# State-space steps of a hybrid decoder layer on one Trainium2 core: two groups' steps taken as one

## The chip, the cores and the metric

The kernel runs on one core of a Trainium2 chip. The metric is the device time of one execution in microseconds (us). Times are medians of several executions; the profile is that of one execution, taken by the hardware profiler. The engines are called PE (matrix products), DVE (vector), ACT (activations), POOL (GpSimd) and SP (which issues most loads). Each takes its instructions in the order in which the program lists them; the weight loads of PE are shown apart, as PEld.

## What is computed

One layer of two parallel branches over a sequence of 1024 positions, width 1024, all in float32. The branch that matters here is a state-space mixer (Mamba-2's dual form) with 8 groups of 4 heads of 64 channels, 128 states and chunks of 128 positions:

```python
def ssd_scan(x, dt, a, bmat, cmat):
    ...
    cb = jnp.einsum('bclgn,bcsgn->bcgls', cc, bc)
    y_diag = jnp.einsum('bcgls,bcgrls,bcsgrp->bclgrp', cb, decay, xd)
    decay_to_end = jnp.exp(a_cs[..., -1:] - a_cs)
    chunk_states = jnp.einsum('bcsgn,bcgrs,bcsgrp->bcgrpn', bc, decay_to_end, xd).astype(jnp.float32)
    ...
    def step(state, inp):
        cs, cd = inp
        return state * cd[..., None, None] + cs, state
    ...
    y_off = jnp.einsum('bclgn,bcgrpn,bcgrl->bclgrp', cc, prev_states, jnp.exp(a_cs))
    return (y_diag + y_off).reshape(b, s, h, p).astype(x.dtype)
```

Afterwards `y_b + xh * d_skip` is multiplied by `silu(ssm_z)` and normed over each group's 256 channels. Both branches are projected, gated, summed, projected again, added to the input and normed.

## The kernel before

The program has one long run of large projections, then the state-space steps, then the projection of the state-space output and the last projection. Large products are done with operands split in a high and a low part (128x512 products of a special 32-bit float type), and with a scheme that needs seven block products for eight.

The change lies in the state-space steps. The work is cut in 32 **steps**: `order` lists them as (group g, piece s), groups in rounds of two, so that steps alternate between the two groups of a round: (0,0) (1,0) (0,1) (1,1) ... (1,3) (2,0) .... A step handles 256 positions, two chunks of 128. Its parts, and the names of tiles by which the profile's rows show them:

- `fetch`: two loads on SP's queue, `dcy` (cumulated decay exponents) and `sl` (the six strips of inputs).
- `mask`, then `decay`: ACT makes `ea` (two instructions), POOL masks `dcy` (an affine select over 128x1024), ACT takes eight exponentials of `dcy`.
- `prep`: PE makes `pc` (products C times B, and B transposed) and `px` (x transposed), eight instructions of 128x128. DVE multiplies `dcy` by `pc` and makes `xd` and `xe` from `px`; ACT copies `bn` out of `pc`.
- `front`: PE does the eight products inside the chunk, `yi`, from `dcy` and `xd` (64-column tiles), and the increments of the state, `sp`, from `xe` and `bn` (one product a chunk). DVE adds the first increment to the state (`add_state`), makes `y` out of `yi` and the skip term (two instructions), and adds the second increment. POOL scales the state before each addition (`mul_state`).
- `back`: PE does the products with states, `yn`. DVE multiplies them by `ea` into `ym`, POOL adds `ym` to `y` and multiplies by the gate strip into `yz`.
- Every second piece of a group, `post` stores `yz`, ACT squares it (`squares`), POOL adds the two strips (`sum`), PE adds over channels with four products of 32-column tiles, `pq` (`post2`), and POOL later takes the root of a small tile `ssq` (`root`).

The last piece of a group (s=3) makes one increment instead of two, and the first (s=0) has no state to scale for its first chunk, so its `ym` and first POOL addition cover half as much.

The other branch's projection, 192 pairs of 128x512 products into `pma`, is the **filler**: `draw(n)` puts n pairs at a place in PE's order. Its evacuations (`tha`) and the low parts of its weights (`wal`) are DVE work that the scheduler places itself.

PE's products keep the order in which the code is written. On DVE, ACT and POOL the helper `link` ties each instruction of a step to the one before it on that engine, so the code's order is the engine's order there too; the other work falls between. All products land in eight PSUM banks of 128x512; the helper `bank` hands out two of them from one ring and six from another, of which the filler's pair holds two for as long as one output block lasts. A bank is written again when the last reader of its former tile is done.

Each step n of the loop before is: `front(n)`; a call that has ACT take the decays of step n+2, POOL scale the state of step n+1 and mask step n+3, and at most one task "beside" (`sum` or `root`); four or five pairs of filler; `back(n)`; `prep(n+2)`; `fetch`.

Of the kernel before, what the change touches and what calls it, by code (L numbers as in the profile page):

```python
# [35 lines left out]
def hybrid_kernel(  # L36
# [1036 lines left out]
    work, last = [], {}  # L1073
# [19 lines left out]
    class Group:  # L1093
# [40 lines left out]
        def prep(self, s):  # L1134
# [10 lines left out]
            xs = []  # L1145
            d3 = dcy.rearrange("p h i l -> p h (i l)")
            link("V", lambda: V.tensor_tensor(d3, d3, pc[:, 0:256].unsqueeze(1).to_broadcast([P, HPG, 256]), op=ALU.mult))  # L1147
            for v, f in (("xd", dthq), ("xe", dde)):
                t = p2x.tile([P, 512], F32, name=f"{v}{nm}", tag=v, bufs=3)
                link("V", lambda: V.tensor_tensor(t.rearrange("p (i h w) -> p i h w", i=2, h=HPG), x4,  # L1150
                                    fac(f, g, s).unsqueeze(3).to_broadcast([P, 2, HPG, HD]), op=ALU.mult))
                xs.append(t)
            bn = p2x.tile([P, 256], F32, name=f"bn{nm}", tag="bn", bufs=3)
            link("A", lambda: A.copy(bn, pc[:, 256:512]))  # L1154
            self.pre[s] = (sl, dcy, bn, xs[0], xs[1], ea)

        def front(self, s):

            g, nm = self.g, f"{self.g}_{s}"
            sl, dcy, bn, xd, xe, ea = self.pre[s]  # L1160
            yi = bank(f"yi{nm}")
# [5 lines left out]
            sp = bank(f"sp{nm}")  # L1167
            two = s < NCH // 2 - 1
            self.sts = [self.st]
            for i in range(2 if two else 1):  # L1170
                mm(sp[:, i * 256 : (i + 1) * 256], bn[:, i * P : (i + 1) * P], xe[:, i * 256 : (i + 1) * 256])
            self.add_state(s, 0, sp)
            if two:
                self.mul_state(s, 1)
            y1 = turn(y1_r, f"y1{nm}", F32).rearrange("p (j t) -> p j t", j=2)
            for j in range(2):
                link("V", lambda: V.scalar_tensor_tensor(y1[:, j], sl[:, 2 + j], dskt[:, 2 * g + j : 2 * g + j + 1],
                                           yi[:, j * 256 : (j + 1) * 256], op0=ALU.mult, op1=ALU.add))
            self.y[s] = y1
            if two:  # L1180
                self.add_state(s, 1, sp)
# [10 lines left out]
        def add_state(self, s, i, sp):  # L1192
# [35 lines left out]
        def post(self, q):  # L1228
# [5 lines left out]
            if g < NG - 2 or q == 0:  # L1234
                later(8, self.squares, q, [yz[:, j] for j in range(2)])
            else:
                self.late = [yz[:, j] for j in range(2)]
                later(5, self.late_squares)
# [12 lines left out]
        def sum(self, q, sq):  # L1251
            link("G", lambda: G.tensor_add(sq[0], sq[0], sq[1]))
            later(3, self.post2, q, sq[:1])
# [58 lines left out]

    def start_ssd():
        fetch(2)
        for n in range(2):
            later(3 + 5 * n, masks, n + 1)
            later(4 + 5 * n, decays, n + 1)
            g, s = order[n]
            later(13 + n, groups[g].prep, s)
# [202 lines left out]
    def ahead_of(n):  # L1522

        with tc.high_priority():
            decays(n + 3)
            if n + 1 < len(order) and order[n + 1][1]:
                groups[order[n + 1][0]].mul_state(order[n + 1][1], 0)
            for _ in range(1 if n < 29 else 2):
                beside_step()
            masks(n + 4)  # L1530

    def step(n, *fs):
        for f in fs:
            item(getattr(groups[order[n][0]], f), order[n][1])

    draw(6)
    for n in range(2):
        step(n, "front")
        ahead_of(n)
        draw(10)  # L1540
    for n in range(len(order)):
        if n > 1:
            step(n, "front")
            ahead_of(n)
            draw(6 if n == 2 else 4 + n % 2)
        step(n, "back")
        if n == 1:
            draw(4)
        if n + 2 < len(order):
            step(n + 2, "prep")  # L1550
        fetch(n + 6)
    while tasks or work:
        draw(2)
        run_tasks()
        beside_step()

# [232 lines left out]
    for u, (nm, k) in enumerate(units):  # L1789
        if k == 0:  # L1790
            if nm == "p1":
                first = {t: psb.tile([P, 512], F32, name=f"{t}p", tag=f"b{t}") for t in ('y1', 'x0', 'x1', 'y3', 'y0', 'x2', 'x3', 'y2')}
# [224 lines left out]
```

## Time and profile before

| What | Value |
| --- | --- |
| Median of 3 executions | 1373.79 us (1373.0 to 1373.83) |
| The profiled execution's own time | 1372.68 us |
| Its span, first to last instruction | 1370.7 us |
| Granted clock of PE | 0.999 |
| PE busy | 1356.4 us |
| Where the 32 steps lie | about 907 to 1118 us |

The profile's page gives the busy time of each engine; "idle before" in a row is how long the engine stood still before the instruction, and the arrow names what ended the wait. In a timeline, rows give start and duration; consecutive instructions of PE, DVE and POOL overlap a little at their ends (the next one starts before the last one's shown end), so what an instruction costs its engine is read from one start to the next.

### The profile page before, as it was taken

Reading aid. Unit: us, or ns where it says so; the run is one execution under the profiler, and the core shown is the slowest. Engines: PE = TensorE matmul, PEld = TensorE weight load, DVE = VectorE, ACT = ScalarE, POOL = GpSimd, SP = SyncE. Lnnn points to the kernel's source line nnn. Section 1 sums busy time; section 2 is a strip of 40 time slices with the busy share of each in tenths; the row PEclk is TensorE's granted clock in tenths of the full one; section 3 lists DMA queues with packets and bytes.
Section 4 is the critical chain, followed back from the end, with each engine's and each line's share of the span. In section 5 each row is a group of like instructions: output and inputs, shape, how many; then the busy total and the mean of one; then the engine's idle time right before and its main releaser. Section 6 shows DMA issues by size and latency. Waiting matters only on the chain.

```text
span 1370.7 us, 20173 instructions
## 1 busy us (share of the span) xinstructions
PE 1356.4 (99%) x6943; PEld 1114.6 (81%) x6943; DVE 1045.6 (76%) x1716; ACT 799.7 (58%) x1447; POOL 192.0 (14%) x191
## 2 busy tenths in 40 slices
PE   8999999999999999999999999999999999999997
PEld 7688888888888888888888888888888878788886
DVE  4786876777778889688897787468878856959976
ACT  5764656666657666466576665486867733333443
POOL 1000000000000000000000000016888871000002
PEclk9999999999999999999999999999999999999999
DMA  9675444333344657777666775489889858978913
GB/s 287 179 234 150 136 123 124 100 122 117 115 132 138 206 172 233 252 239 230 194 198 186 231 239 168 154 314 300 300 284 314 290 203 295 334 267 321 382 38 123
DMA packets 249530, 288.65 MB, mean 211 GB/s; under 512 B 16812, under 2 KB 196436, under 8 KB 249428
## 3 DMA queue, kind: packets, MB, share of 16 engines
q1 hardware_dynamic: 174868, 203.80, 46.3%
q10 hardware_dynamic: 74560, 83.57, 17.9%
q8 instruction: 55, 0.90, 0.3%
q14 instruction: 47, 0.39, 0.1%
HBM read 199.82 MB, written 87.49 MB: 210 GB/s over the span
## 4 chain that ended last, share of the span: by engine, by line
PE 87%; DVE 4%; DMA 3%; POOL 3%; ACT 1%; issue 1%; SPq 1%; POOLq 0%; ACTq 0%; DVEq 0%
PE xcb L565 6%; PE xz L565 6%; PE xx L565 6%; PE xuz L565 6%; PE xg L565 6%; PE pma L82 4%; PE ox L1861 3%; PE yuz L565 3%; PE ycb L565 3%; PE yp L1670 3%; PE yz L565 3%; PE vx L954 3%; PE yx L565 3%; PE yg L565 3%; PE yi L82 2%; PE sp L82 2%
## 5 line engine op out<-in xcount | busy, mean ns | idle before, releaser
L1123 POOL TENSOR_SCALAR_AFFINE_SELECT dcy<-dcy 128x1024 f32<-128x1024 f32 x32 | 35.4, 1106 | 791.5 <-DMA yl<-ya_d 747.2
L1131 ACT ACTIVATE dcy<-dcy,nacs 128x128 f32<-128x128 f32 x256 | 78.3, 389 | 3.6 <-POOL dcy L1123 3.2
L1147 DVE TENSOR_TENSOR dcy<-dcy,pc 128x1024 f32<-128x1024 f32 x32 | 39.0, 1219 | 9.2 <-PE pc L85 5.2
L1226 POOL TENSOR_TENSOR yz<-y,sl 128x512 f32<-128x512 f32 x32 | 43.8, 1369 | 2.5
L82 PE MATMUL pma<-yh,wah 128*128 128x512 f32 x128 | 42.7, 415 | 0.0
L82 PE MATMUL pma<-yh,wal 128*128 128x512 f32 x128 | 42.3, 412 | 0.0
L1154 ACT COPY bn<-pc 128x256 f32<-128x256 f32 x32 | 11.9, 371 | 50.7 <-DVE dcy L1147 48.3
L82 PE MATMUL pma<-yl,wah 128*128 128x512 f32 x128 | 40.1, 394 | 0.0
L1608 DVE SCALAR_TENSOR_TENSOR yn<-yn,par,rb 128x512 f32<-128x512 f32 x32 | 24.3, 760 | 20.6 <-DMA yn<-yb_d 18.8
L1119 ACT ACTIVATE ea<-dcy 64x512 f32<-64x512 f32 x64 | 39.8, 622 | 0.4
L1024 ACT ACTIVATE ac<-ac 128x1024 f32<-128x1024 f32 x32 | 33.9, 1060 | 9.4 <-DVE ac L1022 9.2
L1225 POOL TENSOR_TENSOR y<-y,ym 128x512 f32<-128x512 f32 (+1 forms) x32 | 37.4, 1169 | 2.1 <-DVE ym L1223 2.1
L1223 DVE TENSOR_TENSOR ym<-yn,ea 128x512 f32<-128x512 f32 (+1 forms) x32 | 19.9, 621 | 21.7 <-PE yn L82 21.7
L1022 DVE SCALAR_TENSOR_TENSOR ac<-c2x,cwt,ac 128x1023 f32<-128x1023 f32 (+2 forms) x24 | 30.7, 1279 | 6.3 <-ACT ac L1020 6.2
L82 PE MATMUL yi<-dcy,xd 128*64 128x128 f32 x512 | 35.0, 279 | 0.0
L1022 DVE SCALAR_TENSOR_TENSOR ac<-c2cb,cwt,ac 128x1023 f32<-128x1023 f32 (+2 forms) x24 | 30.6, 1275 | 5.6 <-ACT ac L1020 5.5
L1876 POOL TENSOR_TENSOR r<-r,fnw 128x512 f32<-128x512 f32 x4 | 5.3, 1345 | 206.3 <-ACT junk L1874 206.3
L986 ACT ACTIVATE vm<-vm,vr 128x128 f32<-128x128 f32 x64 | 25.8, 483 | 13.6 <-DMA vm<-v_d 13.1
L824 ACT CAST wbb<-wbr 128x512 fp32r<-128x512 f32 x32 | 19.8, 619 | 22.2 <-DMA wb_d<-wbb 16.2
L82 PE MATMUL sp<-xe,bn 128*128 128x256 f32 x112 | 32.7, 409 | 0.0
L82 PEld LDWEIGHTS yn<-sl,st 128*128 128x128 f32 x224 | 29.8, 191 | 2.8 <-POOL st L1189 0.4
L82 PEld LDWEIGHTS yi<-dcy,xd 128*64 128x64 f32 x512 | 27.3, 136 | 5.7 <-issue 2.9
(2963 smaller groups left out, 4372.6 us busy)
## 6 DMA issues: line engine op xcount, KB each, us to landing
sl<-s_d SPq DMA_DIRECT2D x32, 768.0 KB
s_d<-ac ACTq DMA_DIRECT2D x32, 512.0 KB
wb_d<-wbb ACTq DMA_DIRECT2D x32, 512.0 KB
dcy<-acs_d SPq DMA_DIRECT2D x32, 512.0 KB
av<-in_w_in_dram SPq DMA_DIRECT2D x36, 256.0 KB
aw<-in_ada_w_dram SPq DMA_DIRECT2D x16, 512.0 KB
wbr<-in_w_proj_b_dram SPq DMA_DIRECT2D x32, 256.0 KB
yb_d<-yz ACTq DMA_DIRECT2D x32, 256.0 KB
```

Of the source, the lines that this page charges most:

```text
L82: pin(PE.matmul(acc, l, r, start=first, stop=last))
L565: pin(PE.matmul(ps, lw[:, k * P : (k + 1) * P], r[k], start=first and n + k == 0, stop=n == 2 and k == 3, skip_group_check=not first))
L954: pin(PE.matmul(ps[pn][j], l[:, j * P : (j + 1) * P], r, start=nm in ("p1", "p5", "p2") and n + units[i][1] == 0, stop=n == 2 and k == 3, ...
L1022: V.scalar_tensor_tensor(ac[:, s:], cc[:, : S - s], conv_wt[:, 3 - s, i : i + 1], ac[:, s:], op0=ALU.mult, op1=ALU.add)
L1119: link("A", lambda: A.activation(ea[hh * HD : (hh + 1) * HD], dcy.rearrange("p (j e) i l -> p e j (i l)", e=2)[hh * HD : (hh + 1) * HD, hh ...
L1123: link("G", lambda: G.affine_select(out=d8, in_=d8, compare_op=ALU.is_ge, fill=-1e30, base=0, pattern=[[0, 2 * HPG], [1, P]], channel_mult ...
L1131: link("A", lambda: A.activation(dcy[:, h, i, :], dcy[:, h, i, :], AF.Exp, bias=sub[:, i, h : h + 1]))
L1147: link("V", lambda: V.tensor_tensor(d3, d3, pc[:, 0:256].unsqueeze(1).to_broadcast([P, HPG, 256]), op=ALU.mult))
L1225: link("G", lambda: G.tensor_add(y1[:, :, t0:], y1[:, :, t0:], m[:, :, t0:]))
L1226: link("G", lambda: G.tensor_mul(yz, y1, sl[:, 4:6]))
L1670: pin(PE.matmul(ps[j], a[:, v, js], r, start=first and n + k == 0, stop=n == 2 and k == KT - 1, skip_group_check=not first))
L1861: pin(PE.matmul(ps, a[:, tsl], b[:, cs], start=first and n + j == 0, stop=n == 2 and j == 3, skip_group_check=not first))
```

## The change

Two steps, n and n+1, one of each group of the round, become one. Their parts are written in this order: both `yi` on PE (`inside`); then any `pq` that is due, out of a list `posts`; then both `sp` (`increments`); DVE: `y` of both (`skip`), the first addition of both (`add_state`), and the scaling and second addition of step n alone (`second(n)`); POOL's masks of steps n+3 and n+4. Three pairs of filler follow. Then `each_back`: `back(n)`, **`second(n+1)`**, `back(n+1)`. Then the scaling of both states for the next two steps, `fetch`, and `prep` of both next steps, in which both `dcy` and `xd` come before both `xe`. Six or seven pairs of filler end the double step. ACT takes the decays of steps n+2 and n+3 in a double step. The tasks beside come two at a time. The order of the last part's PSUM banks is adapted.

```diff
+        while posts:
+            p, q, sq = posts.pop(0)
+            p.post2(q, sq)
+        each(n, "increments")
+        each(n, "skip")
+        each(n, "add_state", 0)
+        second(n)
+        masks(n + 5)
+
+    def each(n, f, *a):
+        for m in (n, n + 1):
+            if m < len(order):
+                g, s = order[m]
+                getattr(groups[g], f)(s, *a)
...
+    def second(n):
+        g, s = order[n]
+        if s < NCH // 2 - 1:
+            groups[g].mul_state(s, 1)
+            groups[g].add_state(s, 1)
+
+    def beside(n):
         with tc.high_priority():
-            decays(n + 3)
-            if n + 1 < len(order) and order[n + 1][1]:
-                groups[order[n + 1][0]].mul_state(order[n + 1][1], 0)
-            for _ in range(1 if n < 29 else 2):
+            decays(n + 4)
+            for _ in range(2 if n < 28 else 4):
                 beside_step()
-            masks(n + 4)
-
-    def step(n, *fs):
-        for f in fs:
-            item(getattr(groups[order[n][0]], f), order[n][1])
+    def each_back(n):
+        for m in (n, n + 1):
+            g, s = order[m]
+            groups[g].back(s)
+            if m == n:
+                second(n + 1)
+    def preps(n):
+        each(n, "prep")
+        each(n, "prep2")
+
+    def next_states(n):
+        if n < len(order) and order[n][1]:
+            each(n, "mul_state", 0)
...
     draw(6)
...
+    for n in range(0, len(order), 2):
+        item(fronts, n)
+        beside(n)
+        draw(10 if n == 0 else 3)
+        item(each_back, n)
+        with tc.high_priority():
+            next_states(n + 2)
+        fetch(n + 7)
+        item(preps, n + 2)
+        run_tasks()
+        draw(12 if n == 0 else 6 + n // 2 % 3 % 2)
+        run_tasks()
```

How the instructions stand now is shown at three places of the second round (groups 2 and 3, so tile names begin with the part's letters, the group and the piece; the number after the last underscore only tells buffers apart). First **PE**, at piece 2. Before, one step's products with a strip of squares behind them:

```order
L82 MATMUL yi2_2_9319<-dcy2_2_8989,xd2_2_9211 64x128 x8
L82 MATMUL sp2_2_9328<-xe2_2_9213,bn2_2_9215 128x256 x2
L82 MATMUL pq1_1_9338<-yz1_2_8809,ones_140 32x128 x4
L82 MATMUL pma3_0_9272<-yh10_8034,wal3_0_8946 128x512
L82 MATMUL pma3_1_9275<-yh11_8035,wal3_0_8946 128x512
```

With the change, at the same piece:

```order
L82 MATMUL yi2_2_9317<-dcy2_2_8924,xd2_2_9260 64x128 x8
L82 MATMUL yi3_2_9326<-dcy3_2_9085,xd3_2_9275 64x128 x8
L82 MATMUL pq0_1_9335<-yz0_2_8740,ones_140 32x128 x4
L82 MATMUL pq1_1_9342<-yz1_2_8752,ones_140 32x128 x4
L82 MATMUL sp2_2_9349<-xe2_2_9279,bn2_2_9262 128x256 x2
L82 MATMUL sp3_2_9352<-xe3_2_9281,bn3_2_9277 128x256 x2
L82 MATMUL pma3_0_9299<-yh10_8034,wah3_0_8971 128x512
```

The two groups' `yi` are neighbours now, and the `pq` have moved from behind `sp` to between `yi` and `sp`.

Second **DVE**, at piece 1, from `ym` of group 2 to `ym` of group 3 (`st21` and `st22` are buffers of the state; the addition of `sp3_1` to `st22` is the second increment of group 3's step). Before:

```order
L1223 TENSOR_TENSOR ym2_1_9194<-yn2_1_9189,ea2_1_8837 128x512
L1147 TENSOR_TENSOR dcy2_2_8989<-dcy2_2_8989,pc2_2_9201 128x1024
L1150 TENSOR_TENSOR xd2_2_9211<-px2_2_9200,dthq_154 128x512
L1150 TENSOR_TENSOR xe2_2_9213<-px2_2_9200,dde_155 128x512
L1379 TENSOR_TENSOR wal4_1_9365<-wa4_1_8792,wah4_1_9364 128x512
L1197 TENSOR_TENSOR st_8259<-st_8259,sp3_1_9231 128x256
L1177 TENSOR_SCALAR y13_1_9236<-sl3_1_8906,dskt_151,yi3_1_9222 128x256 x2
L1264 TENSOR_SCALAR cwt_148<-pq0_1_9240 128x128
L1197 TENSOR_TENSOR st22_8262<-st22_8262,sp3_1_9231 128x256
L1223 TENSOR_TENSOR ym3_1_9291<-yn3_1_9286,ea3_1_8908 128x512
```

With the change (the line numbers are those of the changed kernel):

```order
L1205 TENSOR_TENSOR st_8259<-st_8259,sp2_1_9171 128x256
L1205 TENSOR_TENSOR st_8259<-st_8259,sp3_1_9174 128x256
L1205 TENSOR_TENSOR st21_8261<-st21_8261,sp2_1_9171 128x256
L1231 TENSOR_TENSOR ym2_1_9218<-yn2_1_9213,ea2_1_8772 128x512
L1205 TENSOR_TENSOR st22_8262<-st22_8262,sp3_1_9174 128x256
L1231 TENSOR_TENSOR ym3_1_9231<-yn3_1_9226,ea3_1_8923 128x512
L1146 TENSOR_TENSOR dcy2_2_8924<-dcy2_2_8924,pc2_2_9250 128x1024
L1150 TENSOR_TENSOR xd2_2_9260<-px2_2_9249,dthq_154 128x512
L1146 TENSOR_TENSOR dcy3_2_9085<-dcy3_2_9085,pc3_2_9265 128x1024
L1150 TENSOR_TENSOR xd3_2_9275<-px3_2_9264,dthq_154 128x512
```

Eight instructions stood between `ym` of group 2 and the second addition of group 3; now none does, and the `prep` work of the next double step follows behind both `ym`.

Third **POOL**, the same piece (`st22` is scaled here for that second addition). Before:

```order
L1225 TENSOR_TENSOR y12_1_9162<-y12_1_9162,ym2_1_9194 128x512
L1226 TENSOR_TENSOR yz2_0_9045<-y12_1_9162,sl2_1_8835 128x2x256
L1189 TENSOR_TENSOR st22_8262<-st_8259,cd_157 128x256
L1189 TENSOR_TENSOR st_8259<-st21_8261,cd_157 128x256
L1252 TENSOR_TENSOR yz1_2_8809<-yz1_2_8809 128x512
L1123 AFFINE_SELECT dcy2_3_9143<-dcy2_3_9143 128x1024
L1225 TENSOR_TENSOR y13_1_9236<-y13_1_9236,ym3_1_9291 128x512
```

With the change:

```order
L1196 TENSOR_TENSOR st21_8261<-st_8259,cd_157 128x256
L1123 AFFINE_SELECT dcy3_2_9085<-dcy3_2_9085 128x1024
L1123 AFFINE_SELECT dcy2_3_9090<-dcy2_3_9090 128x1024
L1260 TENSOR_TENSOR yz0_2_8740<-yz0_2_8740 128x512
L1260 TENSOR_TENSOR yz1_2_8752<-yz1_2_8752 128x512
L1233 TENSOR_TENSOR y12_1_9177<-y12_1_9177,ym2_1_9218 128x512
L1234 TENSOR_TENSOR yz2_0_9064<-y12_1_9177,sl2_1_8770 128x2x256
L1196 TENSOR_TENSOR st22_8262<-st_8259,cd_157 128x256
L1233 TENSOR_TENSOR y13_1_9180<-y13_1_9180,ym3_1_9231 128x512
```

The scaling of `st22` still stands behind the addition and the product of group 2; ahead of these now stand the scaling of `st21`, two masks and both sums of strips in one row, where before a step had one mask and one sum.

78 lines of the change are left out of this document (36 added, 42 removed).

## The prediction

> **What bounds the kernel now.** I read the page first, then the busy times by stretches, then the timelines of PE, DVE and POOL in the state-space steps. The page's first group gives the busy time of each engine over the span:
>
> ```profile
> PE 1356.4 (99%) x6943; PEld 1114.6 (81%) x6943; DVE 1045.6 (76%) x1716; ACT 799.7 (58%) x1447; POOL 192.0 (14%) x191
> ```
>
> PE is never free, so the time is PE's work, and it falls only if PE does its work with smaller gaps; every stop of PE is added in full, since the filler is a fixed number of pairs. The busy times by stretches (start and end, then busy us and count of PE, PEld, DVE, ACT, POOL) show what stands behind PE in the steps:
>
> ```profile
> 1000.00:1100.00 100.00, 98.97 (x791) 81.98 (x790) 81.39 (x144) 74.29 (x198) 87.50 (x84) 1.00 0.87 299
> ```
>
> DVE is busy 81% and POOL 87%: neither bounds the steps, but neither has much room. One step on PE's timeline (start, duration, instruction):
>
> ```profile
> 937.89 1.05 PE L82 MATMUL yn<-sl,st 128*128 128x128 f32 x8
> 938.78 0.39 PE L82 MATMUL pc<-sl 128*128 128x128 f32 x2
> ...
> 939.11 0.38 PE L85 MATMUL px<-ident,sl 128*128 128x128 f32 x2
> 939.33 0.39 PE L82 MATMUL pc<-sl 128*128 128x128 f32 x2
> ...
> 939.66 0.38 PE L85 MATMUL px<-ident,sl 128*128 128x128 f32 x2
> 939.97 1.09 PE L82 MATMUL yi<-dcy,xd 128*64 128x128 f32 x16
> 941.00 1.13 PE L82 MATMUL sp<-xe,bn 128*128 128x256 f32 x4
> 941.77 0.81 PE L82 MATMUL pma<-yh,wah 128*128 128x512 f32 x2
> 942.42 0.63 PE L82 MATMUL pma<-yl,wah 128*128 128x512 f32 x2
> 942.89 0.62 PE L82 MATMUL pma<-yh,wal 128*128 128x512 f32 x2
> ```
>
> From start to start: `yn` 0.89, `prep` 1.10 (938.78 to the regular end of the last `px`, 0.22 after 939.66), `yi` 1.03, a filler pair 0.46. A strip of squares behind `sp`:
>
> ```profile
> 989.60 1.13 PE L82 MATMUL sp<-xe,bn 128*128 128x256 f32 x4
> 990.66 0.42 PE L82 MATMUL pq<-yz,ones 128*32 128x128 f32 x8
> 991.02 0.73 PE L82 MATMUL pma<-yh,wah 128*128 128x512 f32 x2
> 991.59 0.63 PE L82 MATMUL pma<-yl,wah 128*128 128x512 f32 x2
> ```
>
> DVE and POOL over about one step, late in the steps:
>
> ```profile
> 1049.16 0.87 DVE L1177 SCALAR_TENSOR_TENSOR y<-sl,dskt,yi 128x256 f32<-128x256 f32 x2
> ...
> 1050.80 0.42 DVE L1197 TENSOR_TENSOR st<-st,sp 128x256 f32<-128x256 f32 x1 [0.58 <-POOL st L1189]
> 1052.03 0.69 DVE L1223 TENSOR_TENSOR ym<-yn,ea 128x512 f32<-128x512 f32 x1 [0.81 <-PE yn L82]
> 1052.97 1.22 DVE L1147 TENSOR_TENSOR dcy<-dcy,pc 128x1024 f32<-128x1024 f32 x1 [0.25 <-PE pc L85]
> 1054.11 0.68 DVE L1150 TENSOR_TENSOR xd<-px,dthq 128x512 f32<-128x512 f32 x1
> 1054.71 0.68 DVE L1150 TENSOR_TENSOR xe<-px,dde 128x512 f32<-128x512 f32 x1
> 1055.31 0.41 DVE L1197 TENSOR_TENSOR st<-st,sp 128x256 f32<-128x256 f32 x1
> 1055.63 0.87 DVE L1177 SCALAR_TENSOR_TENSOR y<-sl,dskt,yi 128x256 f32<-128x256 f32 x2
> ```
> ```profile
> 1051.83 1.09 POOL L1123 TENSOR_SCALAR_AFFINE_SELECT dcy<-dcy 128x1024 f32<-128x1024 f32 x1 [0.49 <-ACT ea L1119]
> 1052.89 1.27 POOL L1225 TENSOR_TENSOR y<-y,ym 128x512 f32<-128x512 f32 x1
> 1054.24 1.29 POOL L1226 TENSOR_TENSOR yz<-y,sl 128x512 f32<-128x512 f32 x1
> 1055.80 1.19 POOL L1189 TENSOR_TENSOR st<-st,cd 128x256 f32<-128x256 f32 x2 [0.27 <-DVE st L1197]
> ```
>
> From start to start DVE takes 1.13 for `dcy`, 0.60 for `xd`, `xe` and `ym`, 0.33 for an addition to the state; POOL takes 1.06 for a mask, 1.35 for the addition to `y`, about 1.27 for `yz`, 0.59 for a scaling. The row to keep in mind is DVE's at 1050.80: the second addition waits for POOL's scaling. Over the steps the waits view totals it:
>
> ```profile
> DVE st L1197 <- POOL st L1189: 4.9, 8, 1.4
> ```
>
> 4.9 us in eight waits, little, because five to eight DVE instructions stand between `ym` of one group and that addition, while POOL gets through `y`, `yz` and the scaling.
>
> **What the change takes from PE.** No product is added or removed, only their neighbours change. Between `px` and `yi` the start comes 0.31 after that of `px`, while 939.11 to 939.33 shows 0.22 without a change of tile width: 0.09 for the entry. From `sp` to the second filler pair is 1.42; four records of 256 columns at twice 0.11 (a `yn` record) and one pair make 0.89 + 0.46 = 1.35: 0.07 for the exit. With a strip of squares the same way is 1.99, or 0.57 more, of which 0.36 is `pq` itself: 0.21 for its own entry and exit. A double step pays entry and exit once instead of twice: 16 x 0.16 = 2.6 us. The twelve strips that lie in double steps come in twos between narrow `yi` and `sp`: half of 12 x 0.21 surely goes, perhaps all: 1.3 to 2.5, take 1.9. **Sum 4.5 us**; below it nothing (if every change of width costs what it did), above it all such gaps of before, 32 x 0.16 + 16 x 0.21 = 8.5. One stop of before lies in the steps as well:
>
> ```profile
> 1045.25 0.49 PE L82 MATMUL pc<-sl 128*128 128x128 f32 x2 [0.87 <-DVE st L1197]
> ```
>
> A bank was not free because DVE's addition, behind POOL, was late. With other neighbours it goes, 0.9, or stays.
>
> **What the change adds.** On DVE the second addition of step n+1 now stands right between the two `ym`. It waits for POOL's scaling, which stands behind `y` and `yz` of step n, which wait for `ym` of step n. So DVE stands still for all of POOL's work, and `ym` of n+1, `dcy`, `xd` of the next two steps queue behind it; PE's next `yi` waits for those. Take the end of `yn` of step n as 0, with 0.1 for each handing over (DVE's addition at 1055.31 ends at 1055.72, and POOL's scaling that waited for it starts at 1055.80). `ym` ends at 0.7; POOL: `y` 0.8 to 2.1, `yz` to 3.4, scaling to 4.0; DVE: addition 4.1 to 4.4, `ym` of n+1 to 5.05, `dcy` to 6.2, `xd` to 6.8. **The first `yi` can start at 6.9.** PE meanwhile has `yn` of n+1 (0.89), two `prep` (2.20) and six filler pairs (2.74): it is there at 5.8, or 6.3 with seven pairs. It stops 1.1, or 0.6. Then the second `dcy` and `xd` need 1.13 + 0.60 + 0.1 while the first `yi` runs 1.1: another 0.6.
>
> The other side of POOL: what is queued ahead of `y` of step n. Its row begins with the scaling for the second addition of n, which waits for DVE's first additions, and these come behind four `y` instructions that are late by the same wait. `sp` of n+1 ends 2.3 (three filler pairs, one `yn`) ahead of time 0, the additions 1.3 ahead; scaling and two masks (0.6 + 2 x 1.06) end at 1.4, not at 0.8: 0.6 more. Sums of strips and roots stand there too in some double steps:
>
> ```profile
> L1252 POOL TENSOR_TENSOR yz<-yz 128x512 f32<-128x512 f32 x14 | 18.3, 1306 | 0.0
> L1279 POOL TENSOR_TENSOR ssq<-ssq,nhalf 128x8 f32<-128x8 f32 x6 | 9.9, 1651 | 2.2 <-DMA ssq<-ms_d 2.2
> ```
>
> Two sums are 2.5 us (1.27 from start to start), two roots 3.3. Double step by double step, a round having four, by piece:
> - s=2, four times, no sums ahead: 1.1 + 0.6 + 0.6 = 2.3, once 1.8 (seven pairs): 8.7.
> - s=1: the first round without sums and with seven pairs 1.8; then with two sums 4.8, 4.8 and (seven pairs) 4.3: 15.7.
> - s=0: `ym` and the addition to `y` are half as large (chain 1.1 shorter), `yn` too (PE 0.45 earlier), and the masks are not late, for s=3 before it waits for nothing of this: nothing in the first (twelve pairs), 0.5 in the second, and with two roots ahead 4.3 twice: 9.1.
> - s=3 has no second increment: 0.
>
> Together **33.5 us of PE standing still**. A check from another side, from the last step's `yi`:
>
> ```profile
> 1113.48 1.09 PE L82 MATMUL yi<-dcy,xd 128*64 128x128 f32 x16
> ```
>
> The `yi` at 939.97 is that of the fourth step, this of the 32nd: 28 steps in 173.5 us, 12.4 for two. DVE's work in that is 0.81 x 12.4 = 10.0; with 3.3 of standing behind POOL and 0.4 for the first scaling it is 13.7, against PE's 12.4 - 0.3 = 12.1: 1.6 too much in each of twelve, 19 us, before sums and roots.
>
> Nothing in the rest of the program changes but the banks' order. Moved past the rest are ACT's exponentials and SP's loads: a load comes up to one step later than before, with five sets of buffers behind it, at nothing; a load that is late would show as POOL's mask waiting. Where the second strip of a `prep` gets a bank whose last reader is the late addition, PE stops inside `prep` rather than ahead of `yi`, and has six pairs still to go: it starts again at 4.4, and with half a `prep` and the pairs reaches `yi` at 7.7 instead of 6.9: up to 0.8 more. I take none in the sum and five such places, 4 us, as the upper end.
>
> **Sum, against the profiled execution's own 1372.7** (1.1 below the median of 1373.8, whose time I forecast as the same within that): 1372.7 - 4.5 - 0.9 + 33.5 = 1400.8, **1401 us**.
>
> A page's rule would add to it. First the row, the start of this run, when PE had stood still for 3.5 us:
>
> ```profile
> 3.54 0.45 PE L85 MATMUL pp<-ident,pk 128*128 128x128 f32 x1 [3.54 <-DMA pk<-in_ada_b_dram]
> 3.77 9.78 PE L82 MATMUL pd<-ones,ident 128*128 128x128 f32 x72
> 13.39 0.60 PE L85 MATMUL px<-ident,x 128*128 128x128 f32 x4
> ...
> 19.67 1.95 PE L82 MATMUL pd<-ones,ident 128*128 128x128 f32 x16
> 21.45 0.38 PE L85 MATMUL px<-ident,x 128*128 128x128 f32 x2
> ```
>
> The first 72 records took 9.62 us to the next start (13.39), 0.134 each; the later 16 took 0.111: about 1.6 us lost after a stop of 3.5. The Trainium skill, "TensorE: Matmul & The Clock Gate", section "What's actually happening", says that PE's clock falls to half after an idle window of some 3.4 us and returns after a busy one. By that rule the five long stops of the list could each cost those 1.6 once more; by the rows of the steps they cost nothing beside the wait, but no stop there is so long, so that these rows can't tell.
>
> **Rivals.**
> - *Only the structure waits* (POOL is through its masks, sums and roots in time, for DVE's lateness gives it room): chain 6.9 everywhere: s=2 6.3, s=1 5.8, s=0 2.5, together 14.6: 1382 us. For it: POOL stood idle 12% before. Against it: the sums stand behind a scaling that comes late. 0.20.
> - *The clock falls in the long stops*: 5 x 1.6: 1409 us. For it the start of the run, where a stop of 3.5 us stood ahead of slow records; against it that the stops are little longer than that, and that part of each comes at a second place (the 0.6 at the second `yi`). 0.15.
> - *Faster: the DVE wait is hidden*. PE decides as soon as POOL's three instructions take 2.1 us instead of 3.2, so that `xd` is done at 5.8; then only the gaps count: 1372.7 - 4.5 - 0.9 = 1367 us. For it: spans on POOL are called rough. Against it: DVE's start at 1050.80 comes right at the end that POOL's rows give. 0.06.
> - The change does not do what it says to the gaps: saving 0, 1405; in the forecast's own range.
>
> **How the numbers follow.** Forecast 0.55 (own range 1393 to 1408: the saving's ends, the banks), rivals 0.20, 0.15, 0.06, and 0.04 for what I have not seen, half of it near no change. Range 1379 to 1416, from the first rival with a larger saving to the clock with the banks. About 0.2%, 2.7 us, is what a measurement of this kernel tells from no change: faster 0.06, same 0.02, slower 0.92.
>
> **What would show it.** In the changed kernel's waits, DVE's addition to `st` waiting for POOL's scaling 12 times or more, 40 us or more in all; PE's or PEld's `yi` waiting for DVE's `dcy` or `xd`; POOL idle ahead of a scaling that waits for DVE. The gap between `px` and `yi` 16 times, not 32. PE's busy time no longer 99% between 1000 and 1100. I am wrong if `yi` starts without a stop behind its filler pairs.

## The result, and the profile after

| | before | after |
| --- | --- | --- |
| Median | 1373.81 us (1373.0 to 1374.21, 4 runs) | 1435.13 us (1432.27 to 1436.96, 4 runs) |
| Span of the profiled execution | 1370.7 us | 1434.9 us |
| PE busy | 1356.4 us | 1366.7 us |
| Granted clock of PE | 0.999 | 0.980 |

The changed kernel is slower: ratio 1.0442, 95% interval 1.0423 to 1.0461, or 61 us. The forecast had 27 us. Below, a double step is named by its piece s and its round 1 to 4.

The busy times on the page of after:

```profile
PE 1366.7 (95%) x6943; PEld 1129.3 (79%) x6943; DVE 1046.9 (73%) x1716; ACT 799.0 (56%) x1447; POOL 190.8 (13%) x191
```

The same 6943 records of PE as before, but 10.3 us more of busy time; and span less busy time, PE's idle time, is 68.2 us instead of 14.3. So 53.9 us are PE standing still, and 10.3 us are PE being slower at the same work. The stretch from 1000 to 1100 (columns as in the prediction: start and end, length, then PE, PEld, DVE, ACT, POOL, clock, DMA share, GB/s):

```profile
1000.00:1100.00 100.00, 79.96 (x598) 68.42 (x597) 58.96 (x105) 55.03 (x146) 61.30 (x62) 0.88 0.62 214
```

PE was busy 98.97 of these 100 us before, and every other engine was busier before too: no engine is the bound any more, all wait for each other. The clock column is the second news: 0.88. The waits of after between 900 and 1215 (in all, times, longest), two of the first rows and one further down, and then the second of these rows in the kernel before, between 905 and 1140:

```profile
DVE st L1205 <- POOL st L1196: 47.4, 13, 8.4
POOL dcy L1123 <- ACT ea L1119: 47.0, 13, 18.6
...
PE pc L82 <- DVE st L1205: 16.4, 2, 10.0
```
```profile
POOL dcy L1123 <- ACT ea L1119: 38.3, 18, 18.6
```

The first row is the wait that the forecast is about: DVE's addition behind POOL's scaling, 13 times, 47.4 us, where the kernel before had 4.9 us. The second is one that it had costed at nothing: POOL's mask waiting for ACT. Its total alone says little, since the kernel before had 38.3 us of it. Of the 47.0 us, POOL's timeline has 27.1 in the first steps (before, 22.6 of the 38.3 and 3.7 just ahead of that window), 9.5 in s=3, and 10.4 in s=0 of rounds 2 to 4, and these last are the ones that matter below. PE's longest stops, from its timeline (the bracket is the idle time ahead of the row and what ended it), with three `yi` rows that give the length of double steps:

```profile
983.45 1.97 PE L82 MATMUL yi<-dcy,xd 128*64 128x128 f32 x32
...
997.70 0.79 PE L82 MATMUL pc<-sl 128*128 128x128 f32 x2 [6.42 <-DVE st L1205]
1003.79 1.97 PE L82 MATMUL yi<-dcy,xd 128*64 128x128 f32 x32
...
1016.22 0.69 PE L85 MATMUL px<-ident,sl 128*128 128x128 f32 x2 [3.94 <-DVE st L1205]
...
1066.50 0.79 PE L82 MATMUL pc<-sl 128*128 128x128 f32 x2 [9.98 <-DVE st L1205]
...
1101.84 0.44 PE L85 MATMUL px<-ident,sl 128*128 128x128 f32 x2 [2.18 <-DVE st L1205]
...
1137.83 3.50 PE L82 MATMUL yi<-dcy,xd 128*64 128x128 f32 x32 [8.56 <-DMA dcy<-acs_d]
```

The bracket of the last row names a load, but DVE's addition had waited 8.45 us for POOL until 1132.77, and the `prep` work that this `yi` needs stands behind it. All stops of the steps, by the double step in which the wait arises, against the forecast's list (us):

| piece | measured, rounds 1 to 4 | sum | forecast |
| --- | --- | --- | --- |
| s=0 | 2.2, 6.4, 10.0, 8.6 | 27.2 | 9.1 |
| s=1 | 2.9, 3.9, 4.0, 3.2 | 14.0 | 15.7 |
| s=2 | 1.7, 1.7, 2.2, 2.2 | 7.7 | 8.7 |
| s=3 | 0.5 in round 3 | 0.5 | 0 |
| first `yi` pair, last strips | 2.5, 3.2 | 5.6 | 0 |

s=1 and s=2 came close to the forecast in their sums, and within 1.2 us in each double step; s=0 did not. Here is s=0 of round 2 on SP's queue, ACT and POOL, one view after the other:

```profile
986.85 0.32 SPq L91 DMA_DIRECT2D sl<-s_d  x1
987.27 0.59 SPq L91 DMA_DIRECT2D dcy<-acs_d  x1
```
```profile
992.17 1.27 ACT L1119 ACTIVATE ea<-dcy 64x512 f32<-64x512 f32 x2 [5.78 <-DMA dcy<-acs_d]
```
```profile
988.71 1.09 POOL L1123 TENSOR_SCALAR_AFFINE_SELECT dcy<-dcy 128x1024 f32<-128x1024 f32 x1
993.50 1.09 POOL L1123 TENSOR_SCALAR_AFFINE_SELECT dcy<-dcy 128x1024 f32<-128x1024 f32 x1 [3.70 <-ACT ea L1119]
994.56 0.72 POOL L1233 TENSOR_TENSOR y<-y,ym 128x256 f32<-128x256 f32 x1
...
996.59 0.61 POOL L1196 TENSOR_TENSOR st<-st,cd 128x256 f32<-128x256 f32 x1
```

The load of the rows `dcy` of step n+4 is issued at 987.27, right after that of `sl` of step n+3, which waited for POOL's `yz` of the double step before (its buffer). ACT's `ea` waits 5.78 us, for that load; the mask waits 3.70 us for `ea`; `y`, `yz` and the scaling stand behind the mask; and DVE's addition, which PE's `pc` at 997.70 waits for, behind the scaling.

Last the clock, by stretches of 3.41 us on either side of a fall (clock in the third column from the right), and the sum row over all nine stretches at half clock in the steps:

```profile
936.24:939.65 3.41, 1.17 (x6) 0.70 (x5) 3.41 (x6) 2.67 (x8) 2.17 (x3) 1.00 1.00 367
939.65:943.06 3.41, 3.41 (x12) 2.29 (x12) 1.87 (x4) 3.35 (x8) 0.00 (x0) 0.50 0.95 312
953.31:956.72 3.41, 2.00 (x9) 1.31 (x7) 3.41 (x5) 0.99 (x2) 2.51 (x2) 1.00 0.85 261
956.72:960.13 3.41, 1.88 (x32) 1.76 (x32) 3.32 (x7) 2.45 (x9) 1.19 (x3) 1.00 0.99 354
...
1164.93:1168.34 3.41, 1.42 (x10) 1.34 (x11) 1.90 (x3) 1.19 (x3) 2.28 (x3) 1.00 0.16 61
1168.34:1171.76 3.42, 3.42 (x10) 2.67 (x9) 3.42 (x6) 0.74 (x2) 3.34 (x5) 0.50 0.00 0
```
```profile
sum 54.63, PE 36.84 PEld 31.17 DVE 40.15 ACT 29.42 POOL 32.35; mean PE 4.09 PEld 3.46 DVE 4.46 ACT 3.27 POOL 3.59
```

PE ran at half clock for 54.63 us and was busy in 36.84 of them. If the same work takes half as long at full clock, half of that, 18.4 us, is time lost. By this count the work itself became 1366.7 - 18.4 - 1356.4 = 8.1 us shorter, and 53.9 + 18.4 - 8.1 = 64.2 is the whole difference of the spans.

### The profile page after: what moved, and what is told of

Same layout as the page of the kernel before. It is cut to its first block, busy times and chain, and to the rows that moved or that the text cites. A ratio compares the mean times of both kernels' runs of the same rounds, so it can differ in the third digit from the quotient of the medians.

```text
span 1434.9 us, 20236 instructions
## 1 busy us (share of the span) xinstructions
PE 1366.7 (95%) x6943; PEld 1129.3 (79%) x6943; DVE 1046.9 (73%) x1716; ACT 799.0 (56%) x1447; POOL 190.8 (13%) x191
## 4 chain that ended last, share of the span: by engine, by line
PE 77%; DMA 7%; POOL 6%; issue 4%; DVE 3%; ACT 2%; SPq 1%; POOLq 0%; ACTq 0%; DVEq 0%
PE xx L565 6%; PE xuz L565 6%; PE xcb L565 5%; PE xz L565 5%; PE xg L565 5%; PE ox L1904 3%; PE vx L954 3%; PE yp L1713 3%; PE yx L565 3%; PE yuz L565 3%; PE ycb L565 3%; PE yz L565 3%; PE pma L82 3%; PE yg L565 2%; DMA dcy<-acs_d 2%
## 5 line engine op out<-in xcount | busy, mean ns | idle before, releaser
L1205 DVE TENSOR_TENSOR st<-st,sp 128x256 f32<-128x256 f32 x48 | 19.0, 417 | 52.5 <-POOL st L1196 47.4
L82 PE MATMUL pma<-yh,wah 128*128 128x512 f32 x128 | 45.6, 438 | 4.9 <-ACT dcy L1131 2.2
L82 PEld LDWEIGHTS yi<-dcy,xd 128*64 128x64 f32 x512 | 30.3, 146 | 25.3 <-ACT dcy L1131 10.7
L82 PE MATMUL pma<-yl,wah 128*128 128x512 f32 x128 | 44.5, 431 | 0.0
L82 PE MATMUL pc<-sl 128*128 128x128 f32 x128 | 26.5, 291 | 16.4 <-DVE st L1205 16.4
L1187 DVE SCALAR_TENSOR_TENSOR y<-sl,dskt,yi 128x256 f32<-128x256 f32 x64 | 27.5, 475 | 15.1 <-PE yi L82 10.8
L85 PE MATMUL px<-ident,sl 128*128 128x128 f32 x128 | 26.7, 293 | 12.3 <-DVE st L1205 12.3
L1196 POOL TENSOR_TENSOR st<-st,cd 128x256 f32<-128x256 f32 x48 | 29.8, 631 | 49.9 <-DVE st L1205 44.9
L82 PEld LDWEIGHTS pma<-yh,wah 128*128 128x128 f32 x128 | 25.7, 206 | 11.4 <-ACT dcy L1131 2.6
```

Source lines behind the costliest of these rows:

```text
L82: pin(PE.matmul(acc, l, r, start=first, stop=last))
```

## The experiments

Theory A: the long stops of s=0 come from the late load of a row, by way of ACT's `ea` and POOL's mask. Rival B: they are the structure and the roots. Theory C: the half clock is a loss of its own. All ratios are to runs of the kernel before on the same chip.

| run | median us | ratio, 95% interval | PE idle, profiled |
| --- | --- | --- | --- |
| changed kernel | 1435.1 | 1.0442 [1.0423, 1.0461] | 68.2 |
| e1_mask_behind | 1431.9 | 1.0421 [1.0393, 1.0450] | 63.7 |
| e2_rows_first | 1425.7 | 1.0379 [1.0352, 1.0407] | 59.0 |
| e3_adds_ahead | 1400.1 | 1.0188 [1.0166, 1.0209] | 38.9 |
| e4_warm | 1444.1 | 1.0512 [1.0486, 1.0537] | 41.8 |
| e5_adds_mask | 1405.1 | 1.0237 [1.0223, 1.0251] | 44.8 |
| e6_adds_rows | 1379.4 | 1.0048 [1.0034, 1.0062] | 26.6 |
| e8_warm_half | 1429.8 | 1.0417 [1.0403, 1.0432] | 46.2 |
| e9_sums_behind | 1422.0 | 1.0361 [1.0344, 1.0378] | 57.6 |
| e10_stores_behind | 1381.3 | 1.0060 [1.0047, 1.0073] | 26.5 |
| e11_ends | 1384.3 | 1.0084 [1.0070, 1.0098] | 29.1 |
| e12_roots_last | 1376.7 | 1.0025 [1.0008, 1.0042] | 24.2 |
| e13_pairs_to_end | 1388.6 | 1.0112 [1.0097, 1.0127] | 31.6 |

**e1_mask_behind.**

```diff
 def fronts(n):
     ...
-    masks(n + 5)
+    masks(n + 4)
...
     item(each_back, n)
+    with tc.high_priority():
+        masks(n + 5)
```

> The second of a double step's two masks (step n+4) stands on POOL behind both y and yz instead of ahead of them. Theory A (the three long stops of s=0 in rounds 2 to 4, 6.4, 10.0 and 8.6 us, come because this mask waits for ACT's ea, that for the load of its rows, and that on SP behind a load whose buffer POOL's yz frees late; POOL's y, yz and scaling, and with them DVE's addition, stand behind the mask): these stops fall from 25.0 to 6 or less together, all other stops of s=0 to 2 shrink by the mask's 1.06 (about 6 us), the half-clock stretches behind the long stops go (about 5 us): 1435 - 30 = about 1405. Rival B (the long stops are the roots and the addition's own wait, the mask only passes the time): each stop 1.06 shorter, 1424.

3 us were won instead of 30, and the intervals of the two ratios overlap: a miss. The three long stops of s=0 became 4.7, 12.5 and 5.8: two shrank by 1.8 and 2.8, the middle one grew by 2.5. ACT and POOL in round 3 show why:

```profile
1052.38 0.48 ACTq L1273 DMA_DIRECT2D ms_d<-tri  x1
1052.91 1.27 ACT L1119 ACTIVATE ea<-dcy 64x512 f32<-64x512 f32 x2 [5.08 <-DMA yb_d<-yz]
```
```profile
1054.25 1.09 POOL L1123 TENSOR_SCALAR_AFFINE_SELECT dcy<-dcy 128x1024 f32<-128x1024 f32 x1 [7.62 <-ACT ea L1119]
```

Now the mask of step n+3, which stays ahead of `y`, waits 7.62 us, for an `ea` that starts 0.05 us after the issue of a small store (the means of a strip) is through. Here ACT was held by the issue of a store, and everything behind it was late. Moving one mask on POOL (and its `ea` on ACT, which the same call moves) was not enough: another late `ea` held the mask that stayed. For theory A the run decides little.

**e2_rows_first.**

```diff
 def fetch(n):
+    rest = []
     while done_f[0] < min(n, len(order)):
         ...
         groups[g].fetch(s)
+        rest.append(groups[g].late_load)
...
+    for f in rest:
+        f()
...
 # in the group's fetch(s), behind the load of dcy
-    load(sl, s_d[g][:, s])
+    self.late_load = lambda: load(sl, s_d[g][:, s])
```

> SP issues the loads of the rows dcy of both steps ahead of those of sl, so that the row of step n+4 no longer stands behind a load that waits for POOL's yz. POOL's order stays. Theory A: the mask does not wait any more; the three long stops fall to what the structure and the roots give, 0.5 + 4.3 + 4.3 instead of 25.0: about 1435 - 16 - 2 of the clock = 1417. Rival B: no change, 1435. A second rival: the row's own transfer is late whatever its place (bursts after the idle queue), then the gain is a third or less, 1430.

9.5 us were won; the three long stops of s=0 fell to 2.7, 7.5 and 6.4, the idle time by 9.2. That lies between theory A (18) and the second rival (5). No mask in s=0 waits for `ea` any more (10.4 us before this edit), so the row was late by its place; but with the 2.7 of round 1, 19.3 us of stops stay in s=0, where the forecast had 9.1. PE, POOL and DVE of s=0 in round 3:

```profile
1054.80 0.80 PE L82 MATMUL pc<-sl 128*128 128x128 f32 x2 [7.51 <-DVE st L1205]
```
```profile
1044.21 2.14 POOL L1123 TENSOR_SCALAR_AFFINE_SELECT dcy<-dcy 128x1024 f32<-128x1024 f32 x2
1046.31 3.27 POOL L1287 TENSOR_TENSOR ssq<-ssq,nhalf 128x8 f32<-128x8 f32 x2
...
1051.58 0.62 POOL L1196 TENSOR_TENSOR st<-st,cd 128x256 f32<-128x256 f32 x1
```
```profile
1053.72 0.69 DVE L1395 TENSOR_TENSOR wal<-wa,wah 128x512 fp32r<-128x512 f32 x1 [7.46 <-ACT wah L1390]
1054.33 0.41 DVE L1205 TENSOR_TENSOR st<-st,sp 128x256 f32<-128x256 f32 x1
```

POOL runs without a wait from the masks to the scaling, as in the forecast's chain with two roots, and is done at 1052.20. DVE adds only at 1054.33, because `wal`, a part of the filler's weights, stands ahead and waits for ACT. So 2.1 us of this stop hung on ACT.

**e3_adds_ahead.**

```diff
-    st2 = [... 3 buffers], bn: bufs=3
+    st2 = [... 4 buffers], bn: bufs=2
 def fronts(n):
     ...
-    second(n)
+    for f in ("mul_state", "add_state"):
+        for m in (n, n + 1):
+            ... getattr(groups[g], f)(s, 1)
 def each_back(n):
     ...
-        if m == n:
-            second(n + 1)
```

> Both second additions stand in the first half of the double step (a fourth buffer for the state, one buffer less for the transposed B), so that nothing on DVE between the two ym waits for POOL. If DVE's wait for POOL's scaling is what stops PE: the stops of s=1 (14.0) and s=2 (7.7) go, those of s=0 too, and the clock stays at 1.00: 1435 - 52 - 8 = about 1375. Rival: late masks and loads reach PE by ACT's decays without the addition: 10 to 25 us of stops stay, 1390 to 1400.

35 us were won, 1400: the rival's end, not 1375. The stops of s=1 are gone but for 0.6 in round 4. What stayed: 1.1, 2.9 and 2.8 in s=0 of rounds 2 to 4, 5.5 and 2.2 in s=2 of rounds 2 and 3, 0.3 in s=3 of round 3, 2.5 at the first pair and 8.3 at the end. (The expectations of e5, e6 and e10, below, place all of these in s=0; two of them lie in s=2.) ACT in s=2 of round 2, and PE behind it:

```profile
1008.34 0.50 ACTq L1273 DMA_DIRECT2D ms_d<-cwt  x1
1011.21 0.48 ACTq L1273 DMA_DIRECT2D ms_d<-tri  x1
1011.74 1.27 ACT L1119 ACTIVATE ea<-dcy 64x512 f32<-64x512 f32 x2 [10.38 <-DMA yb_d<-yz]
1013.04 2.44 ACT L1131 ACTIVATE dcy<-dcy,nacs 128x128 f32<-128x128 f32 x8
```
```profile
1010.94 1.09 PE L82 MATMUL yi<-dcy,xd 128*64 128x128 f32 x16
1017.49 1.97 PE L82 MATMUL yi<-dcy,xd 128*64 128x128 f32 x16 [5.46 <-ACT yz L1256]
```

ACT did no arithmetic for 10.38 us and then took the decays that the second `yi` needs (the bracket of that `yi` names another instruction of ACT, which ended at about that time). The late row and the stores reach PE by this way too, with no addition in between.

**e4_warm and e8_warm_half.**

```diff
 def prep(self, s):
     px, pc = bank(...), bank(...)
+    for _ in range({10: 11, 18: 19, 26: 16}.get(order.index((g, s)), 0)):   # e8: 5, 9, 8
+        mm(px, sl[:, 1, 0:P], sl[:, 0:2].rearrange("p a t -> p (a t)"))
```

> Adds 11, 19 and 16 products of 512 columns on PE (about 0.44 us each, 4.8, 8.4 and 7.0 us, written into a bank that is overwritten afterwards, no part of the result) ahead of the two prep in the three double steps with the long stops; PE stood idle there 6.4, 10.0 and 8.6 us. If the half clock behind these stops costs time of its own: the stretches at 0.50 there go, PE's work in them (3.4 + 2.9 + 3.2 us busy) takes half: 4.7 us less, 1430. If the slow work only fills time in which PE would wait anyhow: 1435. If the added work comes onto the path: above 1436.

1444: the added products took 0.86 us each from start to start (11 of them 9.44) and not 0.44, so they did not fit and came onto the path. The run tells nothing of the clock.

> The changed kernel with added products on PE as in e4_warm, with 5, 9 and 8 instead of 11, 19 and 16: one took about 0.88 us, not 0.44, so that e4's did not fit into the stops and its time tells nothing of the clock. These take 4.4, 7.9 and 7.0 us in stops of 6.4, 10.0 and 8.6. If the half clock behind the stops costs time of its own: 3 to 5 us less than the changed kernel's 1435, 1430 to 1432. If it fills time in which PE would wait anyhow: 1435.

1429.8, 5.3 us less than the changed kernel with 22 products more, the fast end of theory C's range. The intervals of the two ratios overlap, so the profile has to carry it. The three double steps in e8, then one of them by its first products:

```profile
985.00:1002.00 17.00, 14.97 (x98) 11.05 (x95) 8.06 (x17) 9.27 (x24) 10.76 (x12) 1.00 0.84 298
1050.00:1070.00 20.00, 17.78 (x98) 12.09 (x98) 10.04 (x19) 9.14 (x25) 12.15 (x12) 1.00 0.95 332
1117.00:1138.00 21.00, 20.17 (x130) 14.37 (x126) 11.64 (x23) 13.27 (x33) 11.68 (x12) 1.00 0.75 275
```
```profile
984.01 1.97 PE L82 MATMUL yi<-dcy,xd 128*64 128x128 f32 x32
...
1002.68 1.53 PE L82 MATMUL yi<-dcy,xd 128*64 128x128 f32 x24
```

The clock is 1.00 in all three, and from `yi` to `yi` it is 18.67 us where the changed kernel took 20.34 (983.45 to 1003.79). The other two are 1.4 and 0.9 shorter, so that the three are 3.9 shorter together, within the 3 to 5 expected. PE's second `prep` starts 14.16 us after `yi` here and 14.25 in the changed kernel, so the stop ends where it did; what is shorter is the work behind it, at full clock. The slow clock cost time of its own.

**e5_adds_mask and e6_adds_rows** are e3 with the edit of e1, and e3 with the edit of e2.

> The kernel with both second additions ahead, and in it ea and the mask of step n+4 moved behind the products with states (ACT's decays of step n+3 then stand ahead of that ea). Theory D (what is left of the stops at yi in s=0, 5.5 + 2.9 + 2.8 and 2.2 us, comes because the decays of step n+3 stand on ACT behind the ea of step n+4, which waits for a late load): these stops go and part of the half clock: 1400 - 13 - 4 = about 1383. Rival E (the two small stores of a strip's squares, which wait on ACT's queue ahead of the decays too, hold them just as long): 1397 or more.

1405, 5 us more than e3: theory D, that the decays are only badly placed, falls; the longest stops at `yi` in rounds 2 and 3 are 6.1 and 7.0.

> The kernel with both second additions ahead, and in it the rows' loads issued ahead of those of sl. If the lateness of the row of step n+4 is what holds ACT in s=0: the stops at yi shrink by the 3 to 5 us that ea waits for it: 1388. If the strips' stores hold ACT whatever the rows do: 1397 or more. Beside e5 this tells apart a late load from a badly placed wait: theory D by place alone gives e5 clearly below e6.

1379.4, 21 us less than e3 and more than was expected. The busy times and the stretch from 1000 to 1100:

```profile
PE 1351.4 (98%) x6943; PEld 1118.1 (81%) x6943; DVE 1048.7 (76%) x1716; ACT 798.3 (58%) x1447; POOL 191.4 (14%) x191
```
```profile
1000.00:1100.00 100.00, 91.82 (x741) 79.69 (x740) 78.06 (x139) 70.04 (x188) 82.96 (x82) 1.00 0.82 290
```

Each of the two edits leaves much of the idle time (59.0 and 38.9 us); with both it falls from 68.2 to 26.6, and the clock in this stretch is 1.00. Against e2, which has the same order of loads, only the additions differ: 59.0 to 26.6, **32.4 us** of idle time. That is the wait that the forecast had priced at 33.5. That the two agree so well is in part chance: e2's stops of s=0 to s=2 come to 41.0 us, and in e6 there are 8.6 of another kind in the steps.

**e9_sums_behind.**

```diff
 def beside(n):
     decays(n + 4)
-    for _ in range(2 if n < 28 else 4):
-        beside_step()
...
     next_states(n + 2)
+    for _ in range(2 if n < 28 else 4):
+        beside_step()
```

> The changed kernel with the sums of strips and the roots on POOL moved behind y, yz and the next scalings, into the time in which POOL waits for DVE's next addition. Theory of the forecast (they stand in the chain at their full 2.5 and 3.3 us): s=1 in rounds 2 to 4 loses 2.5 each, s=0 in rounds 3 and 4 3.3 each, 14 us, and with the half clock about 1418; if the loads of s=0 come earlier too, because POOL's yz in s=3 is 2.5 earlier, 1410. Rival (the sums pass in time in which the chain waits for something else): 1433 to 1436.

1422.0, 13 us less (the profiled execution took 1426.1): the sums and roots were in the chain. The two first `prep` rows behind s=1 and s=0 that answer to 1016.22 and 1066.50:

```profile
1012.59 0.69 PE L85 MATMUL px<-ident,sl 128*128 128x128 f32 x2 [2.18 <-DVE st L1205]
...
1058.19 0.80 PE L82 MATMUL pc<-sl 128*128 128x128 f32 x2 [5.80 <-DVE st L1205]
```

3.94 became 2.18: two sums were worth 1.8 and not 2.5. In s=0 of rounds 3 and 4, with two roots, 9.98 became 5.80 and 8.56 became 3.32, 4.2 and 5.2 less; but in s=0 of round 2, which has neither sums nor roots, 6.42 became 3.37 as well. There it can only be the sums of the s=3 ahead, which had made POOL's `yz` and so the load late. If that part, 3.1 us, is the same in the other two rounds, 1.1 and 2.2 are left for two roots that had been taken at 3.3; the roots were not moved alone.

**e10_stores_behind, e11_ends, e12_roots_last, e13_pairs_to_end** try to bring e6 below the kernel before.

```diff
 # e10 (on e6)
-    send()                        # post2's store on ACT
+    later(2, link, "A", send)
 # e11 (on e10)
-    draw(6); ... draw(10 if n == 0 else 3)
+    draw(11); ... draw(5 if n == 0 else 3)
+    no beside_step() at n == 30
 # e12 (on e6): e11's draws, and two beside_step() instead of four at n == 30
 # e13 (on e12)
-    draw(12 if n == 0 else 6 + n // 2 % 3 % 2)
+    draw(12 if n == 0 else 6)
```

> The kernel with both second additions and the rows' loads ahead, and in it the two small stores of a strip's means on ACT's queue moved behind the decays and squares of the double step. Theory E (the stops that are left at yi in s=0, 2.9 and 2.1 us and some below 1.2, come because ACT's decays of step n+3 stand behind these stores, and a store waits until an earlier transfer is through): these stops go, 1379.4 - 5 = about 1374. Rival F (POOL's mask or a late load is what the decays wait for in any case): 1378 to 1380.

1381.3: no gain. The stop in s=2 of round 2 went (2.9; 0.4 is left, at `sp`), that in s=0 of round 3 stayed, and the end lost what was won:

```profile
1037.58 1.09 PE L82 MATMUL yi<-dcy,xd 128*64 128x128 f32 x16 [2.14 <-ACT bn L1156]
...
1143.94 0.80 PE L1723 MATMUL x3p<-p1bh,p1a 128*128 128x512 f32 x1 [4.73 <-DVE tha L1505]
```

> As e10_stores_behind, and the two ends mended: 11 filler pairs ahead of the first double step instead of 6 and 5 instead of 10 in it (the second yi waited 2.5 us for DVE there), and in the last double step the sums and roots of the round before on POOL behind the last y and yz instead of ahead of them (5.8 us of POOL, against a stop of 3.7 us at the last strips of squares and half a clock of 6.8 us behind it). If these two are stops of the order alone: 2.5 + 1.7 of the clock + 3.7 + 2 of the clock less than e10, 1364 to 1366, below the kernel before. Rival: DVE and POOL are late there by their own work, and only the place of the stop moves: 1372 to 1376.

1384.3, worse than the rival: the first stop shrank (2.5 to 0.4 and 1.0), the end grew to 7.6 us in five stops of over 0.2.

> The kernel with both second additions and the rows' loads ahead (1379.4), and in it 11 filler pairs ahead of the first double step and 5 in it (instead of 6 and 10), and only the two roots (3.3 us of POOL), not the sums, behind the last y and yz. If the two ends are stops of the order: 2.5 + 1.7 of the clock at the start, 3.3 of the 3.7 and 3.4 of the clock at the end less: about 1369, below the kernel before by 0.3%. Rival: as in e11, the stop at the start only moves (0.4 + 1.0 there) and the projection's start then waits for ACT and DVE instead of the strips: 1376 to 1380.

1376.7, the rival's time, 0.25% above the kernel before. The first stop shrank as in e11, the end to 2.0 us, but 8 us of stops stayed in the steps.

> As e12_roots_last, and the five double steps with seven filler pairs behind their prep get six, so that five more pairs (2.3 us) stand at the end, ahead of the last strips. If the end is bounded by its chain (yz, store, squares, sum) and DVE has room in the steps: up to 2 us less than e12, 1367. If DVE's 10.4 us of work per double step and ACT leave no such room: the stops at yi in those five grow by up to 0.46 each and nothing is won, 1369 to 1371.

1388.6: both guesses missed. The last `yi` pair starts 1.7 us later than in e12 although 2.3 us of filler are gone ahead of it, so the steps had no room: 4.0 us. The rest is the end, where the first product of the projection waits for DVE's last `tha`:

```profile
1146.25 0.77 PE L1719 MATMUL x0p<-p1bh,p1a 128*128 128x512 f32 x1 [7.61 <-DVE tha L1501]
```

Why the end moves by several us between these four is not settled. None of them beats the kernel before; e10's and e12's edits together were not tried.

## Why the prediction was wrong, point by point

Slower was right, and the wait named for it is there; but 61 us came instead of 27, outside the range, because two things that the sum held at nothing were not: a late load, and PE's clock.

- **PE as the bound, every stop in full**: right. Where the stops went, the time went with them (e6). 53.9 us of standing and 10.3 of slower work make the whole difference.
- **The saving, 4.5**: 8.1 by the count above, inside the limits that the prediction gave (0 to 8.5). The term for the strips was mis-sized: two `pq` between the two kinds of narrow product cost 0.57 together, what one alone cost before. From e6:

```profile
1101.47 1.97 PE L82 MATMUL yi<-dcy,xd 128*64 128x128 f32 x32 [0.55 <-ACT dcy L1131]
1103.37 0.65 PE L82 MATMUL pq<-yz,ones 128*32 128x128 f32 x16
1103.94 1.99 PE L82 MATMUL sp<-xe,bn 128*128 128x256 f32 x8
1105.59 0.81 PE L82 MATMUL pma<-yh,wah 128*128 128x512 f32 x2
```

  Six such twos save 6 x 0.57 = 3.4 instead of 1.9. The other 4.7 are 0.29 a double step instead of 0.16. Two `yi` take 1.90 here against 2 x 1.03, 0.16 of it; where the rest comes from was not followed.
- **The chain through POOL and DVE**: right in mechanism and close in size. DVE waited 13 times, 47.4 us (forecast: 12 times or more, 40 or more; with the rows first, in e2, it is 38.0); s=1 and s=2 made 21.7 of stops against 24.4; and without that wait the idle time fell by 32.4 (e2 to e6). Where PE meets it came out otherwise: the forecast had `yi` waiting for `dcy` or `xd`, and more than half of the stops (28.7 of 55.0 us) stand inside `prep`, at a bank whose last reader is DVE's late addition.
- **The sums and roots**: in the chain, as e9 shows; two sums 1.8 for 2.5, two roots perhaps 1.1 to 2.2 for 3.3.
- **"A load comes up to one step later than before, with five sets of buffers behind it, at nothing"**: this step failed. There are five sets, but a set's `sl` is only free when POOL's `yz` is through, and on SP the row of step n+4 stands behind it. In s=3, where nothing holds PE, POOL falls behind with two sums, so the load of the next s=0 is late, and its `ea` and mask stand ahead of the work that DVE waits for. Rows first gives 9.5 us by itself and 21 with the additions moved. The prediction's own sign of it, POOL's mask waiting, is there: 10.4 us in s=0 of rounds 2 to 4, and none there with the rows first.
- **s=0, 9.1**: 27.2, and the late load is only 7.9 of the 18.1 too much, for 19.3 stay with the rows first. The other 10.2 are the term itself, mis-sized: 2.7, 2.7, 7.5 and 6.4 in e2 for 0, 0.5, 4.3 and 4.3. One part is known, the 2.1 us behind `wal` in round 3; the rest was not traced to one cause, though it goes with the additions (e6).
- **ACT's queue, "nothing"**: stores whose issue waits hold `ea` and decays (e1, e3). What this costs by itself was not isolated: in e10 one of its stops went without a gain.
- **Banks, none in the sum**: the six stops inside `prep` (four of them are quoted above) come with six or seven pairs still to do. What that adds was not tried by itself; it is within the 32.4.
- **The clock, a rival at 8 us and 0.15**: it happened, nine stretches and 18.4 us. The prediction set the stops that it expected, 4.3 to 4.8 us, against the 3.5 us at the start of the run, and held the fall unlikely because they were little longer and partly split in two. The length of a stop was the wrong measure: stops of 2.2 us were enough. By the Trainium skill, "TensorE: Matmul & The Clock Gate", section "What's actually happening", the clock halves after an idle window of about 3.4 us; the trace agrees in the length of the stretches (3.41, 6.83, 10.24) but not in what brings them about.
- **The ends, nothing**: 5.6 us at the first pair of `yi`, which had ten filler pairs between its two before, and at the last strips, for which there was less cover.

On the spans: forecast -4.5 - 0.9 + 33.5 = 28.1; measured -8.1 + 53.9 + 18.4 = 64.2. Of the 36.1 us between them the clock is 18.4 and s=0 is 18.1; the ends add 5.6, and the larger saving and the shorter stops of s=1 and s=2 take 6.3 back. The forecast's own range, 1393 to 1408, does not follow from the two terms that it names: a saving of 0 to 8.5 and up to 4 us for the banks give 1397 to 1409.

## What to carry to other kernels

When an engine is made to wait in the middle of its queue, follow the wait once round: the engine that comes late frees buffers late, the queue that loads into them is in order as well, and what hangs on that load may stand ahead of the very work that was waited for. Price a stop of PE with the clock behind it: here, over all stops, every 3 us of standing cost 1 us more (53.9 and 18.4). And before an order is given up, look at one in-order queue at a time for what could be moved past: two moved instructions and the changed order of the loads in a double step (e6) took about 55 of the 61 us back.

## What the runs showed of the hardware

The clock of PE falls by a fixed raster of 3.41 us, and not only after a stretch that is wholly idle. In the rows of the raster above, PE was busy 1.17 and 1.42 us of 3.41 and the next stretch ran at half clock; with 2.00 and 1.88 us it did not, though the stop of 2.9 us that lies across these two (up to 958.25) is longer than the others' 2.2 (up to 939.27 and 1166.92). So what counts is how much of one stretch a stop takes. Between 900 and 1200 of after, every stretch at full clock in which PE was busy 1.47 us or less was followed by half clock, and none with 1.64 or more was. The border between is not sharp in the runs: in e9 one with 1.39, from 1121.78 on, was not followed by half clock. When PE works again within a slow stretch, the clock stays at half until its end: behind the stop at 1137.83 the 32 products `yi` took 3.50 us, at 983.45 and 1003.79 they took 1.97.

The issue of a store on ACT can hold ACT's arithmetic for microseconds: in e3 the data of the two small stores were ready on DVE at 1002.2, the stores went out at 1008.34 and 1011.21, and the activation behind them began at 1011.74, after 10.38 us without one. The Trainium skill, "DMA: Bandwidth & Descriptors", section "Anatomy of one DMA — SWDGE (gpsimd) path", on transfers that GpSimd issues, says that a DMA's wait for a semaphore happens on the engine that issues it, before it is sent; these rows of ACT agree. What each store's issue waited for, the rows do not show.
